# A transformer-layer kernel on one Trainium2 core: a fourth buffer for the low halves of the expert table's blocks, and VectorE making every second one

## The chip, the cores and the metric

The program runs on one core of one Trainium2 chip (trn2). The metric is the device time of one execution in microseconds (us). TensorE is PE in the profile (PEld is its weight load), VectorE is DVE, ScalarE is ACT, GpSimd is POOL, and SP is the engine that only starts transfers.

## The reference

One layer works on 512 tokens of 1024 numbers. It adds three residual branches and ends with an RMS norm; the change touches the third, an expert lookup (PEER):

```python
q = (h @ w_query).reshape(B, S, 8, 2, 128)                 # 8 heads, 2 parts
sc = einsum('bshpk,hpnk->bshpn', q, sub_keys)              # 128 keys per part
v1, i1 = top_k(sc[..., 0, :], 16); v2, i2 = top_k(sc[..., 1, :], 16)
cand = v1[..., :, None] + v2[..., None, :]                 # the best 16 of 256 per head
top_s, pos = top_k(cand, 16); idx = take(i1 * 128 + i2, pos); g = softmax(top_s)
act = gelu(einsum('td,tkd->tk', xt, expert_u[idx]))        # 128 experts per token
out = einsum('tk,tkd->td', g * act, expert_v[idx])         # tables of 16384 x 1024
```

## The kernel before

**Precision.** Products in full precision are made of three matmuls of rounded operands: each f32 operand is split into a high half (a rounded copy) and a low half (the rest). For a weight block, `W.fill` loads `w` (512 KB, by SP, line 130), lets ScalarE copy the high half `wh` (line 131), and then one of two makes the low half `wl`: either a transfer ("by DMA": ScalarE writes minus the high part, line 137, and a transfer started by POOL adds `w` to it, line 138), or VectorE subtracts (line 149, in `W.fill_low`). `w`, `wh` and `wl` have three buffers each, taken in turn. `W.get(block)` first fills two blocks ahead. Blocks of the query projection (`pq`) are all made by DMA. Of the blocks of the expert table U, numbers 0 to 25 are made by DMA, 26 to 39 by VectorE.

**Tokens.** The first 128 tokens get their experts' rows by indirect transfers (gathers). For the other 384 the whole tables are multiplied: per block of 128 experts 24 matmuls of 384 columns (`mm1_parts`, lines 111 to 113) give activations, which a dense array of expert weights (`Wd`, in the chip's main memory) multiplies; the second table follows. The first 40 blocks of U (LAG) are done ahead, in the **build**, in which that array of weights is made.

**From the norm to the build.** The stages and their pools of on-chip memory follow each other in the program so: pool `s1` closes; `hp` and `peer` stay; pool `hx` holds the tiles `ht` and `xt` with which the normed tokens are made, turned (32 transposes, line 769) and stored (`x3d<-xt`, four transfers, line 771), and closes; pool `top` opens where `hx` had been closed, with the top values `val`, `idx`, the constants `io2` and `mio` and all tiles of the second level; then pool `qp` opens, with the keys `kr`, the queries `q`, and the scores `sc`. In `qp` 16 query blocks (8 heads x 2 parts) pass: `query(n)` writes `q` from the projection's PSUM bank (line 825 for the first three, whose projections are done before), `key_scores(n)` multiplies it by the keys loaded by `load_keys` (8 matmuls with their loads, lines 819 and 836), and `first_level(n)` finds the best 16 on VectorE (lines 844 to 852). The projection of block n + 1 is asked for ahead of `query(n + 1)` and `key_scores(n)`, from n = 2 on.

**The build.** `second_level(t)` finds the best 16 of each head for 128 tokens (VectorE; its results `sel0`, `sel1` and `gF` are turned by three transposes, line 952). Blocks U0 to U9 stand in the program beside the second level of token tile 1. Then 96 groups make the weights: VectorE makes one-hot arrays `hot` (line 992) and `wei` (line 996), TensorE multiplies them (8 small matmuls, line 1001), ScalarE copies the bank to `stage` (line 1003), and every fourth group is stored to `Wd`. Between groups 2.25 eighths of a U block are put in; `hot` and `wei` have three buffers. U37 to U39 come after the last group, and then the steady stage, an order written out by hand, with second-table matmuls (line 1104).

**Order.** Ahead of the steady stage a planner lays out each engine's order from the program's; at run time each engine takes its instructions in that fixed order and waits where one isn't ready. All PSUM tiles of the parts above share one ring of eight banks (`bank()`).

Of the kernel before, what the change touches and what calls it, by code (L numbers as in the profile page):

```python
# [10 lines left out]
F32 = mybir.dt.float32  # L11
F32R = mybir.dt.float32r
F16 = mybir.dt.float16
BF = mybir.dt.bfloat16
I32 = mybir.dt.int32
# [15 lines left out]
NE = 128  # L31
LAG = 40
# [4 lines left out]
NQ = 3  # L37
NORM_AT = (0, 6), (1, 2)
U_DMA = 3
U_V = range(26, LAG)  # L40
BY_DMA = ("pq",)
G_RATE = 2.45
G_END = 4
# [32 lines left out]
def layer(ctx, tc, a, out, upto=99, dbg=None):  # L76
    nc = tc.nc
    dbg = dbg or {}
    V, A, PE, SP, PL = nc.vector, nc.scalar, nc.tensor, nc.sync, nc.gpsimd

    def pool(stack, name, bufs=1, **kw):
        return stack.enter_context(tc.tile_pool(name=name, bufs=bufs, **kw))
# [3 lines left out]
    wp = pool(ctx, "wp", 3)  # L86
# [5 lines left out]
    def bank(name="bk"):  # L92
        return psum.tile([128, 512], F32, name=name, tag="bk")
# [21 lines left out]
    class Weights:  # L115
# [2 lines left out]

        def __init__(self, plan):
            self.plan, self.raw, self.ready, self.at, self.low, self.used = plan, {}, {}, 0, 0, 0  # L120

        def fill(self, n, cuts=(slice(None),), between=None):
            while self.at < min(n, len(self.plan)):
                key = self.plan[self.at]
                self.at += 1
                src, shape, by_dma = source(*key)
                w = wp.tile(shape, F32, name="w")
                wh = wp.tile(shape, F32R, name="wh")
                for cs in cuts:
                    SP.dma_start(w[:, cs], src[:, cs])  # L130
                    A.copy(wh[:, cs], w[:, cs])  # L131
                    if between:
                        between.pop()()
                wl = None
                if by_dma:
                    wl = wp.tile(shape, F32R, name="wl")
                    A.activation(wl, w, AF.Copy, scale=-1.0)  # L137
                    PL.dma_start(wl, w, accum_op=OP.add)  # L138
                self.raw[key] = w, wh, wl, shape

        def fill_low(self, n, cuts=(slice(None),)):
            while self.low < min(n, len(self.plan)):
                key = self.plan[self.low]
                self.low += 1
                w, wh, wl, shape = self.raw.pop(key)
                if wl is None:
                    wl = wp.tile(shape, F32R, name="wl")
                    for cs in cuts:
                        V.tensor_sub(wl[:, cs], w[:, cs], wh[:, cs].bitcast(F32))  # L149
                self.ready[key] = wh, wl  # L150
# [8 lines left out]
    def source(kind, n):  # L159
# [5 lines left out]
        if kind == "U":  # L165
            return a["U"][n], [128, D], n < LAG - U_DMA and n not in U_V
        if kind == "V":
# [18 lines left out]
    W = Weights(plan)  # L186
# [609 lines left out]
    def mm1_next():  # L796
        ahead[0] += 1
        return mm1_parts(ahead[0] - 1)

    top_pool = ExitStack()  # L800
    tp = pool(top_pool, "top")
    val = tp.tile([128, 8, 2, TT, 16], F32)
    idx = tp.tile([128, 8, 2, TT, 16], U32)

    io2 = tp.tile([128, NE, 2], F16)
    mio = tp.tile([128, 16, 8], F16)
    jr = tp.tile([128, 128], I32)
    PL.iota(jr, pattern=[[1, 128]], base=0, channel_multiplier=0)
    V.tensor_copy(io2, jr[:, :, None].to_broadcast([128, NE, 2]))
    V.tensor_copy(mio, jr[:, :16, None].to_broadcast([128, 16, 8]))  # L810


    with tc.tile_pool(name="qp", bufs=1) as qp:
# [58 lines left out]
    def second_level(t):  # L872


        cand = tp.tile([128, 8, 80], F32, name="cand")
        v0, v1 = val[:, :, 0, t], val[:, :, 1, t]
        V.tensor_add(cand[:, :, :16], v1, v0[:, :, 0:1].to_broadcast(HK))
        V.tensor_add(cand[:, :, 16:72].rearrange("p h (a b) -> p h a b", b=8),
                     v1[:, :, None, :8].to_broadcast([128, 8, 7, 8]),
                     v0[:, :, 1:8, None].to_broadcast([128, 8, 7, 8]))  # L880
        V.tensor_add(cand[:, :, 72:], v0[:, :, 8:], v1[:, :, 0:1].to_broadcast([128, 8, 8]))
        yield
        top = tp.tile(HK, F32, name="tops")
        pos = tp.tile(HK, U32, name="pos")
        for h0 in range(0, 8, 4):
            hs = range(h0, h0 + 4)
            c2 = tp.tile([128, 4, 80], F32, name="c2")
            for h in hs:
                V.max(top[:, h, :8], cand[:, h])
            for h in hs:  # L890
                V.max_index(pos[:, h, :8], top[:, h, :8], cand[:, h])
            yield
            for h in hs:
                V.match_replace(c2[:, h - h0], top[:, h, :8], cand[:, h], LOW)
            for h in hs:
                V.max(top[:, h, 8:], c2[:, h - h0])
            yield
            for h in hs:
                V.max_index(pos[:, h, 8:], top[:, h, 8:], c2[:, h - h0])
            yield  # L900

        p7 = tp.tile(HK, U32, name="p7")
        p3 = tp.tile(HK, U32, name="p3")
        ov = tp.tile(HK, F32, name="ov")
        t0 = tp.tile(HK, F32, name="t0")
        t1 = tp.tile(HK, F32, name="t1")
        rc = tp.tile([128, 2, 16, 8], F16, name="rc")
        V.tensor_scalar(p3, pos, 3, None, op0=OP.logical_shift_right)
        V.tensor_scalar(p7, pos, 7, None, op0=OP.bitwise_and)
        V.tensor_scalar(ov, pos, -72.0, 0.0, op0=OP.add, op1=OP.max)  # L910
        V.tensor_scalar(t0, p3, -1.0, 0.0, op0=OP.add, op1=OP.max)
        V.tensor_scalar(t1, p3, 1.0, 8.0, op0=OP.is_equal, op1=OP.mult)
        V.tensor_add(rc[:, 0].rearrange("p k h -> p h k"), t0, ov)
        V.tensor_add(t1, t1, p7)
        V.tensor_sub(rc[:, 1].rearrange("p k h -> p h k"), t1, ov)
        yield

        out = []
        for p in range(2):
            IK = [128, 16, 16, 8]  # L920
            kn = tp.tile([128, 16, 8], F16, name="kn")
            A.copy(kn.rearrange("p i h -> p h i"), idx[:, :, p, t])
            eq = tp.tile(IK, F16, name="eq")
            V.tensor_tensor(eq, rc[:, p, None].to_broadcast(IK), mio[:, :, None].to_broadcast(IK), op=OP.is_equal)
            yield
            V.tensor_mul(eq, eq, kn[:, :, None].to_broadcast(IK))
            yield
            for m in (8, 4, 2):
                V.tensor_add(eq[:, :m], eq[:, :m], eq[:, m:2 * m])
            dst = tp.tile([128, 128], F32, name="sel%d" % p, bufs=2)  # L930
            V.tensor_add(dst.rearrange("p (h k) -> p k h", k=16), eq[:, 0], eq[:, 1])
            out.append(dst)
            yield

        ex = tp.tile(HK, F32, name="ex")
        su = sm.tile([128, 8], F32, name="su8")
        gF = tp.tile([128, 128], F32, name="gF", bufs=2)
        V.tensor_sub(ex, top, top[:, :, 0:1].to_broadcast(HK))
        A.activation(ex, ex, AF.Exp)
        V.tensor_reduce(su, ex, axis=AX.X, op=OP.add)  # L940
        V.reciprocal(su, su)
        V.tensor_mul(gF.rearrange("p (h k) -> p h k", k=16), ex, su[:, :, None].to_broadcast(HK))
        yield
        if t == 0:
            ib = tp.tile([128, 128], F32, name="ib")
            V.scalar_tensor_tensor(ib, out[0], 128.0, out[1], op0=OP.mult, op1=OP.add)
            V.tensor_copy(gidx, ib)
            V.tensor_copy(gsel, gF)
            return
        pt = bank()  # L950
        for k, src in enumerate((out[0], out[1], gF)):
            PE.transpose(pt[:, k * 128:(k + 1) * 128], src, ident)

        ij = tp.tile([128, 32, 2, 4], F16, name="ij", bufs=2)
        gg = tp.tile([128, 32, 2, 4], F16, name="gg", bufs=2)
        pv = pt.rearrange("p (s g k) -> p s g k", s=4, k=4)
        A.copy(ij[:, :, 0], pv[:, 0])
        A.copy(ij[:, :, 1], pv[:, 1])
        A.activation(gg[:, :, 0], pv[:, 2], AF.Copy, scale=GS)
        V.scalar_tensor_tensor(gg[:, :, 1], pv[:, 2], GS, gg[:, :, 0], op0=OP.mult, op1=OP.subtract)  # L960
        SEL[t] = ij, gg
# [8 lines left out]
    with tc.tile_pool(name="wg", bufs=2) as wg, tc.tile_pool(name="st", bufs=2, side="right") as stages:  # L970
# [7 lines left out]
        rate = (LAG - SPARE - ahead[0]) * NCH / (DT * 32)  # L978
        for tile_ in range(1, TT):
            level = hurried(second_level((tile_ + 1) % TT), OFF2)  # L980
            ij, gg = SEL.pop(tile_)
            for q in range(8):
# [35 lines left out]
        while ahead[0] < LAG - SPARE:  # L1018
            for _ in mm1_next():
                pass  # L1020
        W.fill(W.used + 3)
    top_pool.close()

# [225 lines left out]
```

## Time and profile before

| | us |
|---|---|
| median of 3 runs (1629.12 to 1633.44) | 1630.44 |
| the profiled execution | 1629.31 |
| its span, first to last instruction | 1627.2 |
| outside the span | 2.1 |
| TensorE busy in the span | 1601.2 (98%) |
| VectorE busy in the span | 1257.7 (77%) |

The span covers all engines. Matmuls overlap, so a busy TensorE can still be slower than its best; the granted clock tells when it ran at half speed. Stages on this core: query blocks to about 489 us, build from there to about 723 us, steady stage to the end.

### The profile page before, as it was taken

To read this page: it belongs to the slowest core of one execution; us is meant where nothing else is said; L and a number is where in the kernel's file an instruction comes from. 1 tells how busy PE (TensorE), PEld (TensorE's weight loads), DVE (VectorE), ACT (ScalarE), POOL (GpSimd) and SP (SyncE) were. 2 spreads that over 40 slices of the span, in tenths; PEclk is the share of its full clock that TensorE was granted. 3 is DMA by queue.
4 is the path that set the end of the run, shared out by engine and by line. 5 is a ranking of instruction groups with operands and counts; after the bars stand their busy time and mean duration, and the time that the engine had idled before them with its cause. 6 is when DMAs were issued, how large, how long until landed. Compare 5 with 4: busy or idle time off the path is not lost.

```text
span 1627.2 us, 23635 instructions
## 1 busy us (share of the span) xinstructions
PE 1601.2 (98%) x8512; PEld 1402.5 (86%) x8512; DVE 1257.7 (77%) x2518; ACT 751.4 (46%) x1187; POOL 468.0 (29%) x335
## 2 busy tenths in 40 slices
PE   8999999999998999999999999999999999999997
PEld 6778888888888988899999999999999999988886
DVE  6778884665789999967777777777777777788887
ACT  5468763446446776543333333333333333333334
POOL 0011000001111110025444544445444544453331
PEclk9999999999999999999999999999999999999999
DMA  7344442116777999689989898888898888999993
GB/s 246 117 127 139 128 163 104 65 65 169 205 183 186 254 310 299 228 306 327 311 295 324 286 314 304 305 298 315 294 319 296 304 304 308 309 318 334 316 330 142
DMA packets 155348, 404.76 MB, mean 249 GB/s; under 512 B 13680, under 2 KB 61936, under 8 KB 152160
## 3 DMA queue, kind: packets, MB, share of 16 engines
q1 hardware_dynamic: 110016, 242.36, 43.0%
q0 software_dynamic: 45216, 160.91, 32.0%
q8 instruction: 66, 1.08, 0.3%
q14 instruction: 50, 0.41, 0.1%
HBM read 348.69 MB, written 29.36 MB: 232 GB/s over the span
## 4 chain that ended last, share of the span: by engine, by line
PE 93%; DMA 2%; issue 2%; DVE 2%; ACT 1%; SPq 0%; DVEq 0%; POOL 0%; POOLq 0%; ACTq 0%
PE acc L1104 32%; PE bk L111 17%; PE bk L113 17%; PE bk L112 16%; PE bk L1001 2%; DMA wl<-w 2%; PE pv L111 1%; PE pv L112 1%; PE pv L113 1%; PE om L111 1%; PE om L112 1%; PE om L113 1%; PE bk L836 1%; PE bk L485 1%; PE bk L484 1%
## 5 line engine op out<-in xcount | busy, mean ns | idle before, releaser
L131 ACT CAST wh<-w 128x1024 fp32r<-128x1024 f32 (+1 forms) x333 | 349.4, 1049 | 360.9 <-PE acc L1104 178.2
L111 PE MATMUL bk<-hH,wh 128*128 128x384 f32 (+1 forms) x1128 | 394.2, 349 | 0.0
L113 PE MATMUL bk<-hH,wl 128*128 128x384 f32 (+1 forms) x1128 | 386.8, 343 | 6.5 <-DMA wl<-w 6.5
L112 PE MATMUL bk<-hL,wh 128*128 128x384 f32 (+1 forms) x1128 | 385.2, 342 | 0.0
L149 DVE TENSOR_TENSOR wl<-w,wh 128x1024 fp32r<-128x1024 f32 (+1 forms) x291 | 354.0, 1216 | 25.3 <-ACT wh L131 24.9
L1034 POOL DMA_INDIRECT g<-in_Un,gidx x128 | 207.2, 1619 | 223.3 <-DVE junk L1041 209.3
L1034 POOL DMA_INDIRECT g<-in_V,gidx x128 | 202.4, 1581 | 239.7 <-DVE gacc L1051 225.0
L1104 PE MATMUL acc<-wh,ph 128*128 128x512 f32 x768 | 238.6, 391 | 0.0
L1104 PE MATMUL acc<-wh,pl 128*128 128x512 f32 x768 | 238.2, 391 | 0.0
L1104 PE MATMUL acc<-wl,ph 128*128 128x512 f32 x768 | 238.0, 390 | 0.0
L1081 DVE TENSOR_TENSOR pl<-act,ph 128x384 fp32r<-128x384 f32 x128 | 71.3, 558 | 201.6 <-ACT ph L1078 201.6
L113 PEld LDWEIGHTS bk<-hH,wl 128*128 128x128 f32 x1128 | 212.7, 189 | 12.5 <-DMA wl<-w 8.5
L112 PEld LDWEIGHTS bk<-hL,wh 128*128 128x128 f32 x1128 | 213.0, 189 | 7.0
L111 PEld LDWEIGHTS bk<-hH,wh 128*128 128x128 f32 x1128 | 212.9, 189 | 7.0
L787 ACT ACTIVATE act<-bk 128x384 f32<-128x384 f32 x128 | 63.1, 493 | 279.1 <-PE bk L113 279.1
L1104 PEld LDWEIGHTS acc<-wl,ph 128*128 128x128 f32 x768 | 144.1, 188 | 31.6
L1104 PEld LDWEIGHTS acc<-wh,pl 128*128 128x128 f32 x768 | 144.1, 188 | 31.1
L1104 PEld LDWEIGHTS acc<-wh,ph 128*128 128x128 f32 x768 | 142.9, 188 | 24.3
L1051 DVE SCALAR_TENSOR_TENSOR gacc<-g,gu,gacc 128x1024 f32<-128x1024 f32 x127 | 162.6, 1280 | 0.6
L138 POOL DMA_DIRECT2D wl<-w x42 | 36.1, 859 | 423.0 <-ACT wl L137 391.0
L1041 DVE SCALAR_TENSOR_TENSOR junk<-g,htok 128x1024 bf16<-128x1024 f32 x128 | 156.1, 1220 | 0.8
L111 PE MATMUL bk<-oh,wh 128*128 128x512 f32 x280 | 112.6, 403 | 2.6 <-ACT oh L105 2.6
(306 smaller groups left out, 2126.9 us busy)
## 6 DMA issues: line engine op xcount, KB each, us to landing
w<-in_U SPq DMA_DIRECT2D x128, 512.0 KB
w<-in_V SPq DMA_DIRECT2D x128, 512.0 KB
Wd<-stage SPq DMA_DIRECT2D x24, 1024.0 KB
wt<-Wd SPq DMA_DIRECT2D x90, 256.0 KB
wl<-w POOLq DMA_DIRECT2D x42, 512.0 KB, 5.2
w<-in_w_pq SPq DMA_DIRECT2D x16, 512.0 KB
w<-in_w_in SPq DMA_DIRECT2D x15, 512.0 KB
x<-in_xT SPq DMA_DIRECT2D x16, 256.0 KB
```

The costliest lines, as they stand in the source:

```text
L111: PE.matmul(ps, lh, rh, start=first and c == 0, stop=False)
L112: PE.matmul(ps, lh, rl, start=False, stop=False)
L113: PE.matmul(ps, ll, rh, start=False, stop=last and c == n - 1)
L131: A.copy(wh[:, cs], w[:, cs])
L138: PL.dma_start(wl, w, accum_op=OP.add)
L149: V.tensor_sub(wl[:, cs], w[:, cs], wh[:, cs].bitcast(F32))
L787: A.activation(ACT[e], ps[:, :ND], AF.Gelu_apprx_tanh)
L1034: PL.indirect_dma_start(out=g, out_offset=None, in_=a[table], in_offset=bass.IndirectOffsetOnAxis(ap=gidx[:, k:k + 1], axis=0))
L1041: V.scalar_tensor_tensor(junk, g, 1.0, htok, op0=OP.mult, op1=OP.mult, accum_out=gu[:, st:st + 1])
L1051: V.scalar_tensor_tensor(gacc, g, gu[:, k:k + 1], gacc, op0=OP.mult, op1=OP.add)
L1081: V.tensor_sub(PS[e][1], ACT.pop(e), PS[e][0].bitcast(F32))
L1104: PE.matmul(acc[t, hf], lhs[:, ts], rhs[:, hf * 512:(hf + 1) * 512], start=e == 0 and part == 0, stop=e == NE - 1 and part == 2)
```

## The change

The low halves of U blocks 3, 7, 11, ... (number modulo 4 is 3) go to a fourth buffer, a pool `wx` of one tile opened beside `top`; the others keep taking the three old ones in turn, so that each U block's low half takes the buffer of the block four before it. VectorE now makes the low halves of U11, U13, ... U35 and U37 to U39 (16 in all, before 14), transfers those of the others (24, before 26). `sel0` and `sel1` have one buffer, no longer two, `ib` uses the tile `t0`, and `jr`, from which `io2` and `mio` are copied, moves out of `top` into a pool `ji` of its own, which closes ahead of `qp`. `W.more` is cleared after the last group.

```diff
-U_V = range(26, LAG)
+U_V = *range(11, LAG - U_DMA, 2), *range(LAG - U_DMA, LAG)
...
+            self.more = None
+
+        def low_tile(self, key, shape):
+
+            pool = self.more if self.more and key[0] == "U" and key[1] % 4 == 3 else wp
+            return pool.tile(shape, F32R, name="wl")
...
-                    wl = wp.tile(shape, F32R, name="wl")
+                    wl = self.low_tile(key, shape)
                     A.activation(wl, w, AF.Copy, scale=-1.0)
                     PL.dma_start(wl, w, accum_op=OP.add)
...
-                    wl = wp.tile(shape, F32R, name="wl")
+                    wl = self.low_tile(key, shape)
                     for cs in cuts:
                         V.tensor_sub(wl[:, cs], w[:, cs], wh[:, cs].bitcast(F32))
...
     tp = pool(top_pool, "top")
+    W.more = pool(top_pool, "wx", 1)
...
-    jr = tp.tile([128, 128], I32)
-    PL.iota(jr, pattern=[[1, 128]], base=0, channel_multiplier=0)
-    V.tensor_copy(io2, jr[:, :, None].to_broadcast([128, NE, 2]))
-    V.tensor_copy(mio, jr[:, :16, None].to_broadcast([128, 16, 8]))
+    with tc.tile_pool(name="ji", bufs=1) as ji:
+        jr = ji.tile([128, 128], I32)
+        PL.iota(jr, pattern=[[1, 128]], base=0, channel_multiplier=0)
+        V.tensor_copy(io2, jr[:, :, None].to_broadcast([128, NE, 2]))
+        V.tensor_copy(mio, jr[:, :16, None].to_broadcast([128, 16, 8]))
...
-            dst = tp.tile([128, 128], F32, name="sel%d" % p, bufs=2)
+            dst = tp.tile([128, 128], F32, name="sel%d" % p)
...
-            ib = tp.tile([128, 128], F32, name="ib")
+            ib = t0.rearrange("p h k -> p (h k)")
...
+        W.more = None
         W.fill(W.used + 3)
```

## Rows read from the trace of the kernel before

**Rows 1.** Busy time by stage: engines, granted clock PEclk, DMA share, GB/s
```profile
490.00:540.00 50.00, 45.94 (x251) 44.79 (x250) 48.18 (x248) 33.17 (x44) 8.58 (x10) 0.93 0.79 191
540.00:640.00 100.00, 96.05 (x816) 85.74 (x816) 98.65 (x280) 69.33 (x113) 12.01 (x14) 1.00 1.00 301
640.00:705.00 65.00, 64.97 (x553) 58.81 (x553) 64.80 (x107) 38.57 (x63) 0.00 (x0) 1.00 0.66 244
```

**Rows 2.** TensorE's waits, 480 to 740 us: total us, times, longest
```profile
PE bk L113 <- DMA wl<-w: 6.5, 5, 3.0
```

**Rows 3.** TensorE's timeline in blocks U5 to U7
```profile
516.36 0.34 PE L112 MATMUL bk<-hL,wh 128*128 128x384 f32 x1
519.70 0.69 PE L113 MATMUL bk<-hH,wl 128*128 128x384 f32 x1 [3.00 <-DMA wl<-w]
```

**Rows 4.** Windows of 1 us there; the granted clock is third from the right
```profile
520.00:521.00 1.00, 1.00 (x4) 1.00 (x4) 1.00 (x11) 0.00 (x0) 0.47 (x1) 0.50 1.11 197
526.00:527.00 1.00, 1.00 (x8) 1.00 (x7) 1.00 (x3) 0.51 (x1) 0.00 (x0) 1.00 1.00 401
```

**Rows 5.** VectorE's waits, 498 to 706 us
```profile
DVE hot L992 <- PE bk L1001: 1.0, 2, 0.8
```

**Rows 6.** VectorE at the last group: timeline
```profile
705.06 0.69 DVE L996 TENSOR_TENSOR wei<-hot,gg 128x1024 f16<-128x1024 f16 x1
705.95 1.23 DVE L149 TENSOR_TENSOR wl<-w,wh 128x1024 fp32r<-128x1024 f32 x1 [0.20 <-ACT wh L131]
```

**Rows 7.** TensorE at the last group and the start of U37: timeline
```profile
708.44 0.64 PE L1001 MATMUL bk<-wei,hot 128*128 128x128 f16 x8
710.53 0.33 PE L111 MATMUL bk<-hH,wh 128*128 128x384 f32 x1
```

**Rows 8.** VectorE from 386 to 420 us: waits
```profile
DVE val L844 <- DMA x3d<-xt: 9.9, 1, 9.9
```

**Rows 9.** VectorE from 414 us: timeline
```profile
415.20 0.49 DVE L844 MAX8 val<-sc 128x8 f32<-128x128 f32 x2 [9.94 <-DMA x3d<-xt]
415.95 0.29 DVE L809 CAST io<-jr 128x256 f16<-128x256 int32 x1 [0.26 <-POOL jr L808]
416.16 0.22 DVE L810 CAST mio<-jr 128x128 f16<-128x128 int32 x1
```

**Rows 10.** SP's queue: timeline of its transfers
```profile
387.47 2.33 SPq L819 DMA_DIRECT2D kr<-in_keysT  x4
...
409.46 1.79 SPq L771 DMA_DIRECT2D x3d<-xt  x2
412.80 0.42 SPq L819 DMA_DIRECT2D kr<-in_keysT  x1
```

**Rows 11.** TensorE from 399 us: timeline
```profile
400.05 3.65 PE L769 MATMUL bk<-ident,xT 128*128 128x128 f32 x32
403.55 1.95 PE L836 MATMUL bk<-kr,q 128*128 128x128 f32 x16
405.25 0.48 PE L111 MATMUL bk<-hH,wh 128*128 128x512 f32 x1
...
410.81 1.05 PE L836 MATMUL bk<-kr,q 128*128 128x128 f32 x8
```

**Rows 12.** VectorE's last input of the first transposes of line 952
```profile
517.26 0.38 DVE L931 TENSOR_TENSOR sel<-eq 128x128 f32<-128x128 f16 x1
```

**Rows 13.** TensorE around those transposes: timeline
```profile
534.79 0.34 PE L111 MATMUL bk<-hH,wh 128*128 128x384 f32 x1
534.96 0.38 PE L952 MATMUL bk<-ident,sel 128*128 128x128 f32 x2
```

**Rows 14.** A transfer of 64 KB, and VectorE's wait for it: timeline
```profile
715.79 0.33 SPq L1062 DMA_DIRECT2D wt<-Wd  x1
...
721.38 0.56 DVE L1073 TENSOR_TENSOR act<-act,wt 128x384 f32<-128x384 f32 x1 [3.81 <-DMA wt<-Wd]
```

**Rows 15.** TensorE's busy time from 405 to 488 us
```profile
405.00:488.00 83.00, 83.00 (x421) 70.48 (x419) 66.66 (x451) 39.80 (x57) 11.38 (x14) 1.00 0.79 197
```

## The prediction

> **What bounds the kernel now.** I read the busy time by stage first, then who waited for whom, then the timelines of the places where a wait ends. TensorE sets the end: it is busy in 83.00 of 83 us of the query blocks [rows 15] and in 45.94 of the first 50 us of the build [rows 1], so a delay of TensorE ahead of 489 us moves everything behind it. In the build it waits 6.5 us for low halves that transfers make [rows 2]; the longest, 3.00 us in U6 [rows 3], is followed by some 6 us at a granted clock of 0.50, the lower of the two levels (1.2 GHz), until the row of 526 us shows 1.00 again [rows 4]. What the build gives to be won is thus about 6.5 us of waits and 3 us of clock.
>
> VectorE is nearly full beside it: its busy time in the three build stages is 48.18 of 50, 98.65 of 100 and 64.80 of 65 us [rows 1], 3.4 us of idle time in 215 us, of which 1.0 us is waiting for TensorE to give back a one-hot buffer [rows 5]. So TensorE could go faster in the build only until VectorE holds it.
>
> Two orderings ahead of the build matter for the part of the diff that looks like tidying. First, a pool opened where another lay waits for the whole of the old one. `val` is the first tile written in `top`; its instruction reads scores and touches neither `xt` nor the store, and yet VectorE waited 9.9 us for `x3d<-xt` [rows 8], until 415.20 us [rows 9], when the last of the stores out of pool `hx`, started from 409.46 on [rows 10], had landed. The keys in `qp`, over memory that was free since `s1` closed, were loaded from 387.47 us [rows 10], 28 us earlier. Second, PSUM banks are handed out in the order of the program: the first transposes of the second level had their last input at 517.64 us [rows 12] and ran at 534.96, right behind the first matmul of U9, whose bank the program asks for just ahead of theirs [rows 13].
>
> **The change part by part.**
>
> *The pool `ji`.* `io2` and `mio` are copied from `jr`, so they are its last readers; both lie in `top` and can't be written before 415.20 us [rows 8, 9]. In the change `jr` lies in `ji`, `qp` opens over it, and by the first ordering no key is loaded and no query written before `mio` is done. From the row of `io2` at 415.95 to the end of `mio` at 416.38 is 0.43 us [rows 9], so that is at 415.63. Then SP starts the first key load. Its landing has no row of its own: at least the 0.42 us of starting it [rows 10], at most the 5.6 us between the start of the other transfer of 64 KB at 715.79 and the end of VectorE's wait for it at 721.38 [rows 14]. Neither end is nearer, and I take 3.0, the middle. The first key matmuls then start at 418.6 us, where they started at 403.55 [rows 11]: 15.1 us later (12.5 to 17.7). The queries are no later: VectorE writes them in this time. The Trainium skill, DMA: Bandwidth & Descriptors, Anatomy of one DMA — SWDGE (gpsimd) path, gives a transfer of POOL's about 2.0 us and its bytes at 436 GB/s. For a key load of 64 KB that makes an estimate of 2.15 us, and the sum would be 0.85 us less; no row here shows such a load alone.
>
> Nothing fills that time on TensorE. What it did next is the projection of block 3 (from 405.25 [rows 11]), whose bank the program asks for behind those of the first two key products; by the second ordering it can't pass them. The projections ahead are done at 400.05, where the 32 transposes start [rows 11]. SP holds the key loads until then, but the w load queued behind them feeds a TensorE that stands still as well. VectorE follows with the first level, ScalarE with the copies of the scores.
>
> *The clock behind it.* After 3.00 us of waiting TensorE ran about 6 us (from 519.70 to 526) at 0.50 [rows 3, 4] and lost half of it, 3.0 us. After 15 us of standing still I take the same 3.0, with 0 and twice that, 6.0, as ends. Together 18.1 us (12.5 to 23.7). Nothing takes it back: TensorE is full to 488 us [rows 15], and the second level on VectorE needs all 16 blocks' first levels, each behind its key product.
>
> *The fourth buffer and the new choice of blocks.* With three buffers the low half of U block e + 2 can be begun when block e - 1 is through; with four when e - 2 is through. The high half, which ScalarE copies ahead of it, keeps three buffers, so part of the wait may only change its name. Every second transfer from U12 on goes away while the transfers are at a share of 1.00, and comes back where they were at 0.66 [rows 1]. The waits of rows 2 may all go. But VectorE then sets the pace: two subtractions more, 1.23 us each [rows 6], 2.4 us in all, against 3.4 us of idle time that it can fill; it would be done with `wei` 1.0 us earlier. At the last group TensorE stands 2.7 us behind VectorE (708.44 against 705.06 + 0.69 [rows 6, 7]), and of the 2.1 us from there to U37 at 710.53 [rows 7] some 0.5 are the group's own and 1.6 are U36's last matmuls, which could be done ahead of it; both can shrink to nothing. So the gain is at most 1.0 + 2.7 + 1.6 = 5.3 us, and at worst -2.4, if none of the waits goes. I take 2.5: the bound wants a VectorE without any idle time.
>
> *The rest.* `ib` in `t0` and the pool's `W.more` cost nothing: the same instructions. With one buffer each, `sel0` of tile 2 can't be written before the transposes of tile 1, at 534.96 now [rows 13]; VectorE has other second-level work to put there, and if not it costs up to about 3 us, within the bounds above.
>
> **The sum.** 1629.3 + 18.1 - 2.5 = 1644.9 us for an execution like the profiled one. That one is 1.1 us under the median of the runs, so the median I predict is 1646 us. The bounds: 1629.3 + 12.5 - 5.3 = 1636.5 and 1629.3 + 23.7 + 2.4 = 1655.4, or 1638 and 1656 as medians.
>
> **The rivals.**
>
> *The projections go ahead.* If banks are not what kept the transposes back in rows 13, TensorE can do the projections of blocks 3 and 4 in the gap. One takes 5.6 us (from 405.25 to the next key product at 410.81 [rows 11]); two make 11.1 us, and 15.1 - 11.1 = 4.0 us remain: 1630.4 + 4.0 - 2.5 = 1632 us, with the clock's loss 1635. For it speaks that they need nothing from `qp`; against it the 17 us that the transposes waited with their inputs there [rows 12, 13].
>
> *Not slower: `qp` doesn't wait for `ji`.* If only tiles on the very bytes of a closed pool wait, and `jr` meets none of the early keys, the first part falls away and 1630.4 - 2.5 = 1628 us is left. It decides from the first key load: if that starts near 387 us, this rival is right. Against it is the wait of `val`, which was for the whole of a pool.
>
> *Faster by the full build.* The same, and VectorE loses nothing: 1630.4 - 5.3 = 1625 us. Rows 1 say that VectorE would have to be without a gap for 200 us.
>
> **How the numbers follow.** The forecast has 0.77, the projections ahead 0.09, no wait 0.09, the full build 0.05. What a measurement of this kernel can tell from no change is about 0.3%, 4.9 us: 1625.5 to 1635.3. Faster by more is the last case alone, 0.05; within are the second and third, 0.18; slower is the forecast, 0.77. The range reaches from the projections ahead without the clock's loss, 1632, to 1652: the upper bound of 1656 needs both the longest load and twice the clock's loss. It leaves out the third and fourth case and some 0.04 of the forecast, 0.18 in all.
>
> **What would show it.** Key loads (line 819) that start at about 415.7 us, no longer 387.5; key products (line 836) at about 418.6; a TensorE wait of about 14 us there, put down to the key load or to VectorE's query; a granted clock of 0.50 for some us behind it; U0 at about 507 us, not 489.5. In the build: no wait of TensorE for `wl<-w` above 1 us, more short waits for `wei` and `hot`, VectorE full from the first group to the last, and a build from U0 to U40 that is 2 to 3 us shorter. The prediction is wrong if TensorE has no wait near 404 us, or if it works through the projections there.

## The result, and the profile after

| | before | changed |
|---|---|---|
| median of 4 runs each, us | 1631.6 (1629.1 to 1633.4) | 1649.0 (1646.0 to 1651.7) |
| the profiled execution, us | 1629.31 | 1645.96 |
| its span, us | 1627.2 | 1644.2 |

The ratio of the times is 1.0109 (95%: 1.0091 to 1.0126): slower, by 17 us. The spans differ by 17.0 us as well, and three rows place it: U0 starts at 504.50 us, 15.0 later than before; the first second-table matmul at 744.62, where it was at 727.17, so that the build takes 240.1 us and not 237.7; from there to the end it is 899.6 us, before 900.0. So 15.0 + 2.4 - 0.4. This profiled execution was the fastest of its four.

**The 15 us.** VectorE's timeline of the changed kernel, and SP's queue (lines have moved by 6 to 9: the key load is L827, the key products L844):

```profile
413.92 0.29 DVE L817 CAST io<-jr 128x256 f16<-128x256 int32 x1 [9.46 <-DMA x3d<-xt]
414.13 0.22 DVE L818 CAST mio<-jr 128x128 f16<-128x128 int32 x1
```

```profile
402.64 7.70 SPq L777 DMA_DIRECT2D x3d<-xt  x4
411.32 0.33 SPq L136 DMA_DIRECT2D w<-in_w_pq  x1
414.46 1.76 SPq L827 DMA_DIRECT2D kr<-in_keysT  x4
```

The wait for the stores that `val` had [rows 8] is now that of `io2`, and the key loads, which began at 387.47 [rows 10], begin 0.11 us after `mio` ends (414.13 + 0.22). TensorE's timeline:

```profile
403.52 0.66 PE L775 MATMUL bk<-ident,xT 128*128 128x128 f32 x4 [0.48 <-ACT xt L776]
417.01 3.49 PE L844 MATMUL bk<-kr,q 128*128 128x128 f32 x16 [12.83 <-DMA kr<-in_keysT]
420.26 0.47 PE L111 MATMUL bk<-hH,wh 128*128 128x512 f32 x1
...
504.50 0.42 PE L111 MATMUL bk<-hH,wh 128*128 128x384 f32 x1
...
744.62 0.63 PE L1113 MATMUL acc<-wh,ph 128*128 128x512 f32 x2
```

It stands still for 12.83 us and then runs the 16 key products in 3.49 us, where they took 1.95 [rows 11]. The projection of block 3 follows them; it doesn't go ahead. The windows of 1 us behind the wait (granted clock third from the right):

```profile
418.00:419.00 1.00, 1.00 (x6) 1.00 (x6) 0.00 (x0) 0.00 (x0) 0.00 (x0) 0.50 0.00 0
419.00:420.00 1.00, 1.00 (x7) 1.00 (x6) 0.25 (x2) 0.58 (x1) 0.00 (x0) 0.50 0.00 0
420.00:421.00 1.00, 1.00 (x7) 0.91 (x7) 1.00 (x8) 0.46 (x1) 0.00 (x0) 0.95 0.22 66
```

TensorE works at the lower level for some 3 us, half as long as behind the 3.00 us wait of [rows 3, 4]. From the first key product to U0 it is 87.49 us, before 85.93: the clock cost 1.6 us, the late keys 13.5.

**The build.** Busy time by stage, as in [rows 1] with limits 20 us later, and TensorE's waits from 480 to 740 us:

```profile
510.00:560.00 50.00, 43.54 (x260) 42.37 (x259) 48.95 (x244) 32.78 (x44) 7.48 (x9) 0.93 0.80 202
560.00:660.00 100.00, 97.37 (x830) 87.63 (x827) 96.88 (x215) 65.42 (x107) 6.23 (x8) 1.00 0.82 264
660.00:725.00 65.00, 62.09 (x529) 55.43 (x528) 64.76 (x150) 40.34 (x65) 3.43 (x4) 1.00 0.80 262
```

```profile
PE bk L1009 <- DVE wei L1004: 9.6, 8, 5.9
PE bk L1009 <- ACT wh L137: 1.0, 1, 1.0
PE bk L113 <- DMA wl<-w: 0.6, 1, 0.6
```

The waits for low halves are gone (6.5 us in [rows 2], now 0.6), the transfers are spread evenly (share 0.80 to 0.82), and 9.6 us of waits for `wei` (before 1.4) stand in their place. The longest is ahead of the first group:

```profile
553.57 1.01 PE L1009 MATMUL bk<-wei,hot 128*128 128x128 f16 x8 [5.86 <-DVE wei L1004]
554.34 0.67 PE L111 MATMUL bk<-hH,wh 128*128 128x384 f32 x1
```

Its 8 matmuls take 1.01 us, not the 0.64 of [rows 7]: the clock has fallen again. TensorE came to the first group 5.9 us early, because U0 to U9 had one wait of 0.6 us only, and VectorE's first `wei` is done hardly earlier: 49.0 us after U0 (552.84 + 0.68 - 504.50), before 49.7. Ahead of it stands a subtraction that the new choice gave to VectorE, that of U11:

```profile
551.70 1.22 DVE L155 TENSOR_TENSOR wl<-w,wh 128x1024 fp32r<-128x1024 f32 x1
552.84 0.68 DVE L1004 TENSOR_TENSOR wei<-hot,gg 128x1024 f16<-128x1024 f16 x1
```

In the kernel before, TensorE began the first group 0.14 us after the first `wei` was done (538.47 + 0.69):

```profile
538.47 0.69 DVE L996 TENSOR_TENSOR wei<-hot,gg 128x1024 f16<-128x1024 f16 x1
539.30 0.64 PE L1001 MATMUL bk<-wei,hot 128*128 128x128 f16 x8
```

So the waits of U0 to U9 there (4.0 of the 6.5 us of [rows 2], the longest among them) and the 3 us of clock delayed TensorE little beyond the point at which VectorE would have held it anyway. In all profiles but that of experiment 9 the first `wei` is done 47.5 to 49.7 us after U0, with three buffers as with four.

From the start of the first to the end of the last `wei` VectorE takes 170.8 us, before 167.3: 1.0 us more of work and 2.6 us more of idle time (4.2 us, before 1.6).

```profile
722.96 0.69 DVE L1004 TENSOR_TENSOR wei<-hot,gg 128x1024 f16<-128x1024 f16 x1
```

Most of that idle time is one wait, for ScalarE, which waits for a store of weights:

```profile
594.96 1.09 ACT L1011 ACTIVATE stage<-bk 128x512 f32<-128x512 f32 x2 [6.47 <-DMA Wd<-stage]
...
597.55 0.33 ACT L967 ACTIVATE gg<-bk 128x128 f16<-128x128 f32 x1
```

```profile
597.90 0.29 DVE L968 SCALAR_TENSOR_TENSOR gg<-bk,gg 128x128 f16<-128x128 f32 x1 [2.94 <-ACT gg L967]
```

The copy of `gg` had its input from 593.1 us on and stood in ScalarE's queue behind a copy to `stage`.

### The profile page after: what moved, and what is told of

Read it like the earlier page. It is cut to its first block, busy times and chain, and to the rows that moved or that the text cites. A ratio compares the mean times of both kernels' runs of the same rounds, so it can differ in the third digit from the quotient of the medians.

```text
span 1644.2 us, 23653 instructions
## 1 busy us (share of the span) xinstructions
PE 1602.2 (97%) x8512; PEld 1402.8 (85%) x8512; DVE 1260.7 (77%) x2520; ACT 750.1 (46%) x1185; POOL 466.7 (28%) x333
## 4 chain that ended last, share of the span: by engine, by line
PE 84%; DVE 12%; DMA 2%; ACT 1%; issue 1%; SPq 0%; DVEq 0%; ACTq 0%
PE acc L1113 31%; PE bk L111 14%; PE bk L112 14%; PE bk L113 14%; DVE hot L1000 2%; DVE wei L1004 2%; DVE wl L155 1%; PE pv L111 1%; PE pv L112 1%; PE pv L113 1%; PE om L111 1%; PE om L112 1%; PE om L113 1%; PE bk L844 1%; PE bk L1009 1%
```

## The experiments

Times are medians of 4 to 12 runs; ratios are to the kernel before, run on the same chip, where its medians were 1631.3 to 1632.6 us. "Build" is from U0 to the first second-table matmul in the one profiled execution (before 237.7 us).

**1. The pool alone.** The kernel before with

```diff
-    jr = tp.tile([128, 128], I32)
+    with tc.tile_pool(name="ji", bufs=1) as ji:
+        jr = ji.tile([128, 128], I32)
...
```

`io2` and `mio` are copied inside the pool.

> The kernel before with one edit of the change: jr moves into the pool ji, which closes ahead of qp. Theory (qp waits for ji, and ji's readers wait for the last store out of hx): first key load at about 414.5 us, first key products at about 417, TensorE idle for 13 us ahead of them, U0 15 us later than before, the build from U0 to U40 as long as before (233.5 us), the time 15 us above the kernel before, about 1646.5. Rival (the fourth buffer's pool beside top, not ji, delays the keys): key loads near 387 us, key products near 403.5, time as before, 1631.6.

Measured: 1647.1 us, 1.0093 (1.0077 to 1.0109). SP's queue and TensorE:

```profile
416.42 6.43 SPq L820 DMA_DIRECT2D kr<-in_keysT  x6
```

```profile
418.99 3.50 PE L837 MATMUL bk<-kr,q 128*128 128x128 f32 x16 [13.97 <-DMA kr<-in_keysT]
...
506.49 0.42 PE L111 MATMUL bk<-hH,wh 128*128 128x384 f32 x1
```

U0 is 17 us late (this execution came to the wait some 1 us later, and it was 1.1 us longer); from the keys to U0 87.50 us, as in the changed kernel. The build takes 237.9 us, as before. The pool makes nearly all of the loss.

**2. The change without the pool**, `jr` in the ring of `c2`:

```diff
-    with tc.tile_pool(name="ji", bufs=1) as ji:
-        jr = ji.tile([128, 128], I32)
+    jr = tp.tile([128, 4, 80], I32, name="c2").rearrange("p a b -> p (a b)")[:, :128]
```

> The changed kernel with the one edit taken back: jr shares the ring of the second level's tile c2 in top, no pool ji; the fourth buffer, the new choice of blocks, the single sel buffers and ib stay. Theory: key products at 403.5 us again, U0 at 489.5; the build keeps its 2.4 us (236 us from U0 to U40), because VectorE sets its pace with two subtractions more; the time 2 to 3 us above the kernel before, about 1634. Rival 1 (the fourth buffer's pool delays the keys): 1646 or more. Rival 2 (the build was longer only because the delay shifted it against the transfers): build of 231 us, time about 1629.

Measured: 1632.9 us, 1.0012 (1.0002 to 1.0021). Key products at 403.23 us, U0 at 489.16, build 240.65 us. The stall is the pool's, the build's 2 to 3 us are not, and they don't come from the delay.

**3. The pool on other memory**: the changed kernel with

```diff
-    with tc.tile_pool(name="ji", bufs=1) as ji:
+    with tc.tile_pool(name="ji", bufs=1, side="right") as ji:
```

> The changed kernel with one word added: the pool ji opens at the other (right) side of the on-chip memory, so that jr's copies stand where they stood in the program and ji still closes ahead of qp, but qp's place isn't ji's. Theory (qp waits because it is opened over the bytes that ji held): key loads near 387 us, key products near 403.5, U0 near 489.5, time as without ji, about 1633. Rival (a closed pool, or the order of the program, holds what is opened next wherever it lies): key products near 417, time as the changed kernel, 1647 to 1649.

Measured: 1633.3 us, 1.0009 (0.9999 to 1.0018). SP and TensorE:

```profile
388.80 2.60 SPq L827 DMA_DIRECT2D kr<-in_keysT  x4
```

```profile
404.88 1.95 PE L844 MATMUL bk<-kr,q 128*128 128x128 f32 x16
```

The same pool, opened and closed at the same places of the program, costs nothing where `qp` doesn't get its bytes.

**4. A projection asked for earlier**, in the changed kernel:

```diff
-            if NQ <= n + QAHEAD < 16:
-                PQ[n + QAHEAD] = proj(("pq", n + QAHEAD), ho)
+            for m in ([3] if n == 0 else [n + 1] if 3 <= n < 15 else []):
+                PQ[m] = proj(("pq", m), ho)
```

> The changed kernel, with the projection of query block 3 asked for ahead of the first key products (those of blocks 4 to 15 where they were). Theory (TensorE idles there because banks and instructions keep the program's order, with work at hand that needs nothing from qp): the projection runs from 404 to 409.7 us, 7 us of idle time stay, key products at 417 as in the changed kernel, U0 some 5.5 us earlier than there, about 499; the time 3 to 5.5 us less than the changed kernel's, about 1644 to 1646, less than 5.5 if VectorE, which starts its first level at 419.75 still, then holds the build. Rival (the projection waits for something of qp or for its weights): no change, 1649.

Measured: 1648.2 us, 1.0103 (1.0087 to 1.0119). TensorE, SP's loads, and POOL:

```profile
405.31 0.50 PE L111 MATMUL bk<-hH,wh 128*128 128x512 f32 x1
...
421.50 5.16 PE L844 MATMUL bk<-kr,q 128*128 128x128 f32 x24 [10.43 <-DMA kr<-in_keysT]
```

```profile
413.06 0.33 SPq L136 DMA_DIRECT2D w<-in_w_pq  x1
416.30 2.75 SPq L827 DMA_DIRECT2D kr<-in_keysT  x4
```

```profile
413.92 0.85 POOL L144 DMA_DIRECT2D wl<-w  x1 [6.57 <-ACT wl L143]
```

The projection did run in the gap, so it was the program's order that kept it out. The gain was missed, though: U0 at 504.51 us. From the keys to U0 it is 83.0 us, 4.5 less, but the keys landed 5.2 us after their load was started, not 2.55, and that start was 1.8 us later than in the changed kernel, where the transposes had ended 1.3 us earlier. The load of weights ahead of the keys isn't new: it starts 3.2 us ahead of them here and 3.1 us there (411.32 and 414.46). New is a transfer of 512 KB for a low half, which POOL starts ahead of the keys; in the changed kernel it starts none between 405.20 and 429.07 us. The transfers' share behind the start of the keys was 0.74 to 1.10 for four windows of 1 us (416 to 420), there 0.43 to 0.79 for three (414 to 417). That this transfer slowed the key load is likely and wasn't tried.

**5. The fourth buffer with the old choice** (as 2, with `U_V = range(26, LAG)`).

> As the run without the pool ji, and the choice of blocks is that of the kernel before (VectorE subtracts for U26 to U39, 14 blocks, not 16): the fourth buffer alone. Theory (VectorE sets the pace of the build): two subtractions of 1.23 us less than with the new choice, so 2.5 us faster than that, about 1631.5, within 2 us of the kernel before, TensorE's waits for low halves mostly turned into waits for wei. Rival (transfers set the pace, and only the new choice relieves them): waits for wl of 5 us or more stay and the time is above that with the new choice, 1635 or more.

Measured: 1633.7 us, 1.0016 (1.0001 to 1.0031); waits for `wl` 0.9 us. The rival's waits are absent; but with two subtractions less it isn't faster than 2 (0.8 us slower, within the intervals), where the theory wanted 2.5 us less.

**6. The new choice alone**: the kernel before with

```diff
-U_V = range(26, LAG)
+U_V = *range(11, LAG - U_DMA, 2), *range(LAG - U_DMA, LAG)
```

> The kernel before with one edit of the change: VectorE subtracts for U11, U13 ... U35 and U37 to U39 (16 blocks, not the last 14); three buffers, no pool ji. Theory (VectorE sets the pace, and the fourth buffer only renames waits): as the run without the pool ji, which had four buffers, about 1633, 1 to 3 us above the kernel before; TensorE's waits for wl smaller than 6.5 us, since transfers and subtractions alternate. Rival (the new choice needs the fourth buffer: with three, a subtraction late on VectorE keeps a buffer from the next transfer): waits for wl of 8 us or more and 1636 or more.

Measured: 1628.6 us, 0.9978 (0.9970 to 0.9987), the fastest kernel here: it beats the kernel before by 0.22%, less than the 0.3% that I named, and 2 by 0.34%. Both expectations fell on the time (the waits for `wl` were 5.2 us), and with three buffers the two extra subtractions were thus no loss. Its profiled execution was the slowest of its twelve (1631.85 us, build 240.8), so where the others gained isn't seen.

**7. Fewer subtractions**, as 2, with 9 blocks on VectorE, then with 3, in place of 16:

```diff
-U_V = *range(11, LAG - U_DMA, 2), *range(LAG - U_DMA, LAG)
+U_V = *range(13, LAG - U_DMA, 4), *range(LAG - U_DMA, LAG)
...
+U_V = range(LAG - U_DMA, LAG)
```

> As the run without the pool ji (four buffers), with fewer subtractions on VectorE: U13, U17 ... U33 and U37 to U39, 9 blocks, not 16. VectorE has 7 x 1.22 = 8.5 us less to do up to U40, 7 more blocks go through transfers. Theory (VectorE alone sets the pace of the build): its waits fall away as far as TensorE lets them: U0 to U37 some 5 us shorter than with 16 subtractions (224.0 there), time about 1628. Rival (transfers are the second bound: their share was 1.00 over 100 us of the kernel before, and ScalarE waited 6.5 us for one store of weights in the changed kernel): no gain, waits of ScalarE for stage and of TensorE for wl grow, 1633 or more.

> The same with 3 blocks only on VectorE (U37 to U39): 13 x 1.22 = 15.9 us less than with 16. Theory (VectorE alone): U0 to U37 shorter by the 7 us that TensorE could give, time about 1626. Rival (transfers are the second bound): the transfers' share stays at 1.00 through the groups, VectorE gets 10 us or more of idle time, TensorE waits for wl again, 1635 or more.

Measured: 1631.3 us, 1.0001 (0.9987 to 1.0014) with 9, and 1640.1 us, 1.0058 (1.0038 to 1.0079) with 3. The groups from 540 to 700 us with 16, and then with 3:

```profile
540.00:700.00 160.00, 155.00 (x1306) 139.13 (x1306) 155.32 (x354) 101.68 (x163) 10.28 (x12) 0.99 0.81 261
```

```profile
540.00:700.00 160.00, 154.88 (x1297) 139.53 (x1296) 146.90 (x345) 107.12 (x170) 20.57 (x24) 0.98 0.97 289
```

With 3, VectorE is idle for 13 us, TensorE is no busier, and the transfers' share has gone from 0.81 to 0.97. TensorE doesn't wait for `wl` (0.6 us in all): the wait is ScalarE's, from 489 to 720 us:

```profile
ACT stage L1010 <- DMA Wd<-stage: 42.3, 12, 8.3
```

With 16 these waits were 8.9 us. So VectorE doesn't set the pace alone: 8.5 us less work gave 1.6 us, which the intervals don't tell from nothing, and 15.9 us less cost 7.2.

**8. Nine blocks with three buffers** (the kernel before with that choice).

> The kernel before with 9 blocks subtracted by VectorE (U13, U17 ... U33, U37 to U39), three buffers, no pool ji. The same choice with four buffers measured 1631.3, 16 blocks with three 1628.6. Theory (VectorE's pace, and the fourth buffer costs some us): between 1625 and 1629, TensorE's waits for wl some 5 us. Rival (with three buffers each transfer's wait falls on TensorE, and transfers are the bound as soon as VectorE has fewer blocks): 1631 or more, waits for wl above 7 us.

Measured: 1634.8 us, 1.0021 (1.0012 to 1.0031), waits for `wl` 7.6 us: the rival. Against 7 with 9 blocks it is 3.5 us slower, though the intervals touch. The two kernels differ in the savings of memory as well, so that isn't the fourth buffer alone.

**9. Two more blocks ahead of the groups**, as 2, with `U_MID = 12`.

> As the run without the pool ji (four buffers, new choice, 1632.9), and U0 to U11 stand beside the second level of token tile 1 (U0 to U9 there), so that TensorE has 8.3 us more of matmuls before the first group. Theory (VectorE sets the pace; TensorE's wait of 5.5 us for the first wei and the 6 us at a clock of 0.50 behind it are idle time that VectorE leaves it anyway): the wait goes, the clock stays at 1.00, and the time stays within 1.5 us of 1632.9. Rival (the gathered wait and the lower clock behind it are what the fourth buffer costs): 4 to 5 us faster, about 1628.5.

Measured: 1631.3 us, 0.9993 (0.9982 to 1.0003). It told nothing of the wait, which didn't go: VectorE's first `wei` moved as well, to 550.14 us (537.49 in 2), and TensorE waited 6.7 us for it.

**10. The savings of memory added to 6**, with one buffer each for `sel0` and `sel1` and `ib` in `t0`.

> The kernel before with the new choice of blocks, and with the change's savings of memory: one buffer each for sel0 and sel1, ib in t0. Three buffers for low halves, no pool ji. The new choice alone measured 1628.6, with the fourth buffer and these savings 1632.9. Theory (the fourth buffer itself costs those 4 us): as the choice alone, 1627.5 to 1630. Rival (the single sel buffers cost them: ScalarE's copy of gg kept VectorE waiting 2.8 us in that run): 1632 to 1634.

Measured: 1635.4 us, 1.0019 (1.0007 to 1.0031), 7 us above 6. Which of the savings costs it isn't shown. In the profile (1639.38 us, the second slowest of twelve) VectorE waits twice for `ex`, 4.8 and 4.9 us; the first time, ScalarE and then VectorE:

```profile
628.14 1.06 ACT L137 ACTIVATE wl<-w 128x1024 fp32r<-128x1024 f32 x1 [3.26 <-DMA w<-in_U]
629.22 1.28 ACT L939 ACT_TABLE_LOAD   x1
630.51 0.31 ACT L939 ACTIVATE ex<-ex 128x128 f32<-128x128 f32 x1
```

```profile
630.85 0.29 DVE L940 TENSOR_REDUCE su<-ex 128x8 f32<-128x128 f32 x1 [4.77 <-ACT ex L939]
```

The exponential's input was written from 623.12 on; it stood behind the first step of a low half that waited for its load.

**11. All of the change but the pool and the single buffers**: 2 with two buffers each for `sel0` and `sel1`, the memory found by writing `t1` over `p3`.

```diff
-            dst = tp.tile([128, 128], F32, name="sel%d" % p)
+            dst = tp.tile([128, 128], F32, name="sel%d" % p, bufs=2)
-        t1 = tp.tile(HK, F32, name="t1")
+        t1 = p3.bitcast(F32)
```

> The changed kernel without the pool ji and with two buffers each for sel0 and sel1 again (the memory comes from t1, which is written over p3, whose last reader is t1's own instruction): fourth buffer and new choice. Theory S (the single sel buffers cost the build 4 to 7 us, as 1635.4 against 1628.6 says, and the fourth buffer is worth 1 to 2): 1626 to 1628.5, faster than both kernels, and faster than the new choice alone. Rival 1 (the fourth buffer itself is worth nothing): 1628.6, as the choice alone. Rival 2 (not the buffers of sel: any shift of ScalarE's short copies behind a late load makes such differences): 1631 to 1635.

Measured: 1632.9 us, 1.0005 (0.9996 to 1.0014). Theory S, drawn from 10, fell; the time lies in the range of rival 2, which isn't yet its cause. The profile has a build of 237.6 us, 3.1 shorter than in 2, but U0 at 493.87 us. ScalarE and TensorE at the last query block:

```profile
489.62 1.06 ACT L143 ACTIVATE wl<-w 128x1024 fp32r<-128x1024 f32 x1 [4.74 <-DMA w<-in_U]
...
491.51 0.58 ACT L834 COPY q<-bk 128x512 f32<-128x512 f32 x1
```

```profile
492.14 2.08 PE L843 MATMUL bk<-kr,q 128*128 128x128 f32 x8 [2.86 <-ACT q L834]
493.87 0.67 PE L111 MATMUL bk<-hH,wh 128*128 128x384 f32 x1
```

The fourth buffer lets the first step of a low half (L143) come ahead of the last query's copy, and when its load is late, the copy, TensorE and the clock (0.50) pay: from the first key product to U0 89.1 us, 85.9 before. With the fourth buffer this wait stands ahead of that copy in all nine profiles, 2.1 to 4.7 us long; it reached TensorE with more than the usual 0.5 us in four without the pool `ji` (up to 2.9 us). With three buffers ScalarE waits no more than 0.8 us for a load here.

## Why the prediction was right, and where it was not

- **`qp` waits for `ji`, which waits for the stores.** Shown, by 1, 2 and 3: the pool costs 16 us alone, nothing on other memory. The late start of the keys was predicted as 15.1 us and measured 13.5 (12.5 to 17.7 were the bounds). The key load began at 414.46, not 415.63, and its landing, taken as 3.0 us, took 2.55. The estimate from the Trainium skill, DMA: Bandwidth & Descriptors, Anatomy of one DMA — SWDGE (gpsimd) path, was 2.15 us (its figures are for POOL's transfers, the key load is SP's) and fell about as short (0.4 us) as mine was long; experiment 4 gave 5.2 us for the same load, which no constant would have given. Whether all of `qp` waits, or only the tiles that lie on `jr`'s bytes, the runs don't tell: SP starts its transfers in order, and a first key load that waits holds the others.
- **Projections can't fill the gap.** Right: TensorE stood still for 12.83 us, and in 4 the projection ran in the gap once the program asked for it ahead of the keys. The rival in which they go ahead is out, and so are the two in which `qp` doesn't wait.
- **The clock behind it, 3.0 us (0 to 6).** Right in kind, mis-sized: 1.6 us, since TensorE worked at the lower level for 3 us here, and for 6 in the row from which I took it. Together 15.0, not 18.1.
- **The fourth buffer and the choice: -2.5 us (-5.3 to 2.4).** This step failed, in sign: +2.4 us in the profile, 2.0 us in 2 (0.3 to 3.4) and 1.5 us in 3 (-0.2 to 2.9). A gain of 2.5 us is out by both intervals; that it is a loss is barely clear of the noise. Its first half held: with the fourth buffer TensorE waits 0.4 to 1.1 us for `wl` in all nine profiles, with three 4.4 to 7.7 in all five. What failed was "VectorE then sets the pace", with idle time that it can fill. The last `wei` should have been done 1.0 us earlier; counted from U0 it was done 2.9 us later (219.2 us, before 216.3). VectorE didn't fill its idle time but had more of it, 4.2 us between the first and the last `wei`, of which 2.9 us is the wait for ScalarE's copy of `gg`. And of the 2.7 + 1.6 us in which TensorE stands behind VectorE at the end, 0.45 us went (it begins the last group at 725.89 us, 2.24 us behind VectorE). That makes the 2.4 us. 7 showed that less work for VectorE hardly helps; with 3 blocks ScalarE's waits for stores and the transfers' share rise in its place, which points to them as the next bound. A small slip besides: the transfers go away from U11 on, not U12.
- **The number.** The time of 1649.0 us lies 3 us from the forecast of 1646, and in the range of 1632 to 1652. That it came so near is partly luck, since the error of 4.9 us in the build and that of 3.1 us in the stall were of opposite signs; either alone would have left it in the range.
- **The single `sel` buffers: "up to about 3 us".** I left them inside the bounds. Build 240.65 against 237.6 us (2 and 11) agrees with that size, 10 against 6 gives 7 us, and the times of 2 and 11 give none.

**What stays open.** The parts of the build's change don't add up: the choice alone is 3 us faster, with the savings 3 slower, with savings and fourth buffer 1 to 2 slower, with the fourth buffer but two `sel` buffers (11) as fast as before. The times of one kernel spread by 3 to 13 us (1631.3 to 1634.4 for 2, 1630.4 to 1643.6 for 5), and one profile of each can't place differences of 2 us. That short copies behind a waiting ScalarE carry them is seen in three profiles, and not tried by moving them.

## What to carry to other kernels

A small pool for a passing tile isn't free: what opens next over its bytes waits for its last reader, and through that for whatever the reader waits for; put it where nothing early will lie, as one word did here (16 us). A buffer that removes a wait is worth only what the next bound leaves (here the longest waits lay ahead of a point at which VectorE would have held TensorE anyway); count all engines near the full (here TensorE, VectorE and the transfers) before taking the wait's length as the gain. More buffers also let instructions that wait for loads move forward in a queue: look at which short instruction stands behind them, and who needs it.

## What the runs showed of the hardware that was not expected

A longer wait wasn't followed by longer work at the lower clock: 3.00 us of waiting by 6 us [rows 3, 4], 12.83 us by 3 us, and the 5.86 us ahead of the first group of the changed kernel, too, by 3 us (from 553.57). The windows show that the clock fell while TensorE stood still, and how long it had been low when the work began: in the 12.83 us wait it shows 0.50 from 407 us on, 10 us ahead of the first key product; in the 5.86 us wait from 550 us on, 3.6 us ahead of the first group; in the 3.00 us wait the window of 519 us, in which the work begins, is the first below 1.00 (0.55).

```profile
407.00:408.00 1.00, 0.00 (x0) 0.00 (x0) 0.00 (x0) 0.33 (x1) 0.00 (x0) 0.50 1.15 438
...
550.00:551.00 1.00, 0.00 (x0) 0.00 (x0) 1.00 (x2) 1.00 (x2) 0.00 (x0) 0.50 0.37 148
...
555.00:556.00 1.00, 1.00 (x5) 1.00 (x4) 1.00 (x3) 0.22 (x1) 0.00 (x0) 0.50 0.72 254
556.00:557.00 1.00, 1.00 (x7) 0.84 (x7) 0.53 (x1) 0.00 (x0) 0.00 (x0) 0.69 0.78 299
557.00:558.00 1.00, 1.00 (x13) 0.93 (x10) 0.46 (x1) 0.46 (x1) 0.00 (x0) 1.00 0.87 270
```

And the same load of 64 KB was there after 2.55 us in one order of the transfers, and after 5.2 us in another in which a transfer of 512 KB had been started 2.4 us ahead of it.
